# A hybrid GLA and pooling block on one core: column tiles 4 and 5 of r as a second Strassen unit, the feature sums begun earlier

## The chip, the core and the metric

The kernel runs on one core of a Trainium2 chip. The core has a matrix engine (TensorE; PE in the profile, its weight loads PEld), a vector engine (VectorE; DVE), a scalar engine (ScalarE; ACT), GpSimd (POOL) and a sync engine (SyncE; SP) that here issues the DMA transfers. The engines run beside each other and wait for one another at semaphores. SBUF is the on-chip memory with 128 partitions; PSUM is the accumulator memory of TensorE, used here as eight banks of 128 x 512 floats.

The metric is the device time of one execution in microseconds (us), as the median of several runs. The kernel before takes 1376.15 us (three runs: 1376.15, 1376.6 and 1376.02).

## The reference

One transformer-like block on a sequence of 1024 tokens with 1024 channels, in float32:

```python
h = rmsnorm(x, norm_mix)
q, k, v, r, lr_f, lr_b, u, g_a, g_b = split(h @ w_in)        # r: 1024 columns, u: 512, gates: 1024 each
o = gla_forward(q, k, v, decay(lr_f)) + gla_backward(q, k, v, decay(lr_b))   # 4 heads
o = per_head_rmsnorm(o) * gla_norm
o = o * silu(r)
y_a = o @ w_branch_gla
y_b = grouped_linear(multiscale_pool(u)) * pool_scale
merged = sigmoid(g_a) * y_a + sigmoid(g_b) * y_b
x = x + merged @ w_out
gate, up = split(rmsnorm(x, norm_ffn) @ w_ffn_in)
x = x + (silu(gate) * up) @ w_ffn_out
return rmsnorm(x, norm_final)
```

The change lies in the projection h @ w_in, in how the columns of r are computed, and in the preparation of h for it.

## The kernel before

**Numbers as pairs.** Every float32 operand of a matmul is held as two parts, hi (the value cast to the matmul's format) and lo (the rest). A product of two operands is three matmuls, hi x hi, hi x lo and lo x hi (`products`, `mm3`, line 273 does all of them). ScalarE makes hi by a cast (L200) and VectorE or GpSimd makes lo by a subtraction (L201). `hT` is h transposed, features on partitions: for four pairs of k-tiles and two token halves a slot of hi and a slot of lo (`hh`, `hl` in the profile).

**Straight tiles.** `feature_major` computes one column tile of 128 columns for one half of the tokens (512): 8 k-tiles x 3 matmuls, so 48 for both halves. `order` lists the weight tiles that are used this way: q and k of each head, then column tiles 0 to 5 of r. `fetch`, `prepare` and `take` load them, split them and hand them out.

**Strassen units.** Other columns of w_in are computed in units of two column tiles (`Unit`, L1069), as a 2 x 2 block product by Strassen's method in Winograd's form: seven products of 4 k-tiles x 3 matmuls instead of eight. The weights of a unit are two loads of 512 KB (`fraw`), their four combined sums are made on VectorE (`fs`, L1089), and `step(p)` splits the operand of product p. On the other side stand blocks of hT (products 1, 2, 3) and four sums of blocks (products 4 to 7). Products 1, 6, 7, 4 accumulate in one bank, 5 and 3 in another, 2 in a third; after products 1, 6 and 5 ScalarE copies a bank out (`ga`, L1467), and the results of 2, 3, 7, 4 come from VectorE additions to these copies. Before, `gate_units` has 11 units: one of r (column tiles 6 and 7), two of u, four of each gate. `Ahead` prepares the weight operands in the order of use; `R_RUN` is the order of products of the unit of r, 1, 2, 6, 5, 3, 7 and 4, of which 4 is done during the next unit.

**The feature sums.** The four sums of blocks of hT are made early and parked in DRAM. `feature_sums(c)` (L643) restores h from hi + lo on VectorE, takes differences, and stores them to `f_out`; `feature_parts` (L665) loads each back (`hs`), ScalarE casts it (`trh`, L707) and VectorE takes the rest (`trl`, L698). Both run as jobs of `prepare_beside`, which starts one step each `every` units of `mm3` work (one unit is one `mm3` of 512 columns), and only while no weight split is pending. Stores of sums go out three steps after they were made (`PUT`).

**What sets the order.** Each engine executes in the order in which the program issues. The schedule is written out by hand: `pump`, called after every `mm3`, advances first steps put off (`soon`), then weight splits, then `aside` (the jobs beside), then `side` (generators: normalization, transposing features, attention). `finish_side` and `finish_beside` drain these queues. In `first_qk` (L1035) the second half of the tokens is still being transposed in `side` while the first half of q and k is computed; then `low_rank(1)` is run and the feature sums are begun.

**Gated output.** `gated(j, half, src)` (L1178) takes a column tile of r: silu on ScalarE (`sr`), four transposes of the attention output into a bank (`tp`, L1184), and one VectorE instruction that multiplies them into `oT`. After four such calls on a pair of column tiles the two slots of oT are stored. The attention output of heads 0 to 2 was stored to DRAM and is loaded back by `load_o(h)` (`ol`, L1033, two slots of 512 KB); head 3's is still in SBUF. r tiles 0 to 2 are copied out (`whole_r`) and gated later by `put_by`, one half at a time, since the attention of head 3 is then not done.

**Slots.** All large tiles (hT, sums, `fraw`, `ol`, `oT`, `ga`, `trh`, `trl`) come from one pool of 39 slots of 128 x 1024 floats, handed out in turn. An instruction that writes a new tile waits until every user of the slot's former tile is done. SP issues its DMAs in program order, so a load that waits for a slot holds back those behind it.

In the stage of the change the kernel runs: the last attention steps beside r tiles 0 to 3, r tiles 3 to 5 with `put_by` and `gated`, then the loop over `gate_runs` (L1515). The functions and loops named here follow.

Of the kernel before, what the change touches and what calls it, by code (L numbers as in the profile page):

```python
# [53 lines left out]
def kernel(  # L54
# [42 lines left out]
    def slot(dtype=F32, shape=(2, HALF), s="slot"):  # L97
        return slots.tile([P, *shape], dtype, tag="slot", name=name(s))
# [136 lines left out]
            return tuple(t[:, k % self.per, :] for t in self.parts[k // self.per])  # L235


    order = []
    for h in range(HEADS):
        order += [(w_in, KT, c + h * DK, DK) for c in (Q0, K0)]  # L240
    order += [(w_in, KT, R0 + j * P, P) for j in range(KT - 2)]
    order = iter(order)
    loaded, ready = [], []

# [398 lines left out]
    def feature_sums(c):  # L643
# [18 lines left out]
        yield job  # L662
        yield diff(b21, b21, b22, 4)

    def feature_parts():  # L665
        todo = [(p, c) for p in (6, 5, 7, 4) for c in range(2)]
        wholes = []

        def load_sum():
            if len(wholes) < len(todo):  # L670
                p, c = todo[len(wholes)]
                wholes.append(slot(s="hs"))
                nc.sync.dma_start(wholes[-1][:, :, :], f_out[p][:, c])

        yield load_sum, None, None
        for n, (p, c) in enumerate(todo):
            yield load_sum, wholes[n][:, :, :], p

    def parts_for(src):
# [350 lines left out]
    def load_o(h):  # L1030
        o_heads[h] = [slot(shape=(4, DV), s="ol") for _ in range(2)]
        for half in range(2):
            nc.sync.dma_start(o_heads[h][half][:, :, :], o_out[h][:, 4 * half : 4 * half + 4, :])  # L1033

    def first_qk():  # L1035
        q, k = slot(s="q"), slot(s="k")
        low_rank(0)
        weights = [take()]
        for half in range(2):
            if half:  # L1040
                finish_side()
                low_rank(1)
                prepare_beside([feature_sums(0)], 2)
                prepare_beside([feature_sums(1)], 4)
                prepare()
            for n, (dst, scale) in enumerate(((q, DK**-0.5), (k, 1.0))):
                if n == len(weights):
                    weights.append(take(ahead=False))
                ps = feature_major(weights[n], hT, half)
                nc.scalar.activation(dst[:, half, :], ps[:, :], AF.Copy, scale=scale)  # L1050
        qk_heads[0] = q, k
# [104 lines left out]
    def product(unit, p, ps, right):  # L1156
# [6 lines left out]


    ob_out = {(i, half): dram.tile([P, 4, HALF], F32, name=f"ob_out{i}{half}") for i in range(2) for half in range(2)}
    gate_units = [(R0 + 6 * P, R0 + 7 * P)] + [(U0 + 2 * i * P, U0 + (2 * i + 1) * P) for i in range(2)]
    gate_units += [(c0 + 2 * i * P, c0 + (2 * i + 1) * P) for c0 in (GA0, GB0) for i in range(KT // 2)]
    gunits = [Unit(w_in, cols) for cols in gate_units]
    gate_runs = [run_of(n, 0) for n in range(len(gate_units))]
    gate_runs[0] = [(0, p) for p in R_RUN[:-1]]  # L1170
    gate_runs[-1] = last_run(len(gate_units) - 1)
    gates_ahead = Ahead(
        gunits, [(0, p) for p in R_RUN] + list(chain(*(steps_of(n, n == len(gate_units) - 1) for n in range(1, len(gate_units)))))
    )

    raw_r, oT = [], {}
# [27 lines left out]
            gated(*raw_r.pop(0))  # L1204

    BY = 3
    sums_begun = False
    for j in range(KT - 2):
        if 2 <= j <= 4:
            load_o(j - 2)  # L1210
        w = take()
        if j == 4:
            for _ in range(2):
                gunits[0].load()
        if j == 5:
            gates_ahead.step()
        if j < BY:
            whole_r = slot(s="r")
        for half in range(2):
            if j >= BY and not sums_begun and (j > BY or not side):  # L1220
                finish_side()
                finish_beside()
                prepare_beside([feature_parts()], 5)
                sums_begun = True
            ps = feature_major(w, hT, half)
            if half == 0:
                flush()
            if j < BY:
                nc.scalar.copy(whole_r[:, half, :], ps[:, :])
                raw_r.append((j, half, whole_r[:, half, :]))  # L1230
            else:
                put_by()
                gated(j, half, ps[:, :])
            if j == KT - 3 and half == 0:
                gates_ahead.step()
    for p, i, half in ((1, 0, 0), (2, 1, 0), (3, 1, 1)):
        right[p] = [hT.pair(2 * i + c, half) for c in range(2)]

# [206 lines left out]
    class Gates:  # L1445


        def __init__(self, n):
            self.unit = gunits[n]
            self.kind, self.at = next((kind, n - at) for kind, at in (("b", 7), ("a", 3), ("u", 1), ("r", 0)) if n >= at)  # L1450
            self.rows, self.done = [], []

        def row(self, i):
# [4 lines left out]
        def run(self, p):  # L1458
            while len(right.get(p, ())) < 2:
                next(aside[0][0])  # L1460
            ps = bank_of(self, p)
            product(self.unit, p, ps, right)
            ps = ps[:, :]
            finish_late()
            part = {1: (0, 0), 6: (0, 1), 5: (1, 1)}.get(p)
            if part:
                nc.scalar.copy(self.row(part[0])[:, part[1], :], ps)  # L1467
                return
            i, half = {2: (0, 0), 3: (0, 1), 4: (1, 0), 7: (1, 1)}[p]
            done = self.row(i)[:, half, :]  # L1470
            if p != 4:
                add(done, ps, done)
                ps = done
            if self.kind == "r":
                if p == 4:
                    nc.scalar.copy(done, ps)
                late.append(partial(gated, KT - 2 + i, half, done))
                return
            if self.kind != "u":
                nc.scalar.activation(done, ps, AF.Sigmoid)  # L1480
            elif p == 4:
                nc.scalar.copy(done, ps)
            self.done.append((i, half))
            if self.kind == "b" and p in (7, 4):
                for at in self.done:
                    self.pooling(*at)
                self.done = []
# [27 lines left out]
    for n, run in enumerate(gate_runs):  # L1515
        zs[n] = Gates(n)
        last = n == len(gate_units) - 1
        if n == 1:
            prepare_beside(map(output_jobs, range(4)), 2.8)
        if n == 8:  # L1520
            finish_side()
            finish_beside()
            prepare_beside(map(unit_jobs, range(READY)), 2.8, 0, 2)
        for at, (of, p) in enumerate(run):
            if not gates_ahead.step() and at in (5, 7):
                line_make()
            zs[of].run(p)
            for _ in range(2 * (at == 0 and not last)):
                gunits[n + 1].load()
            if p in (7, 4):  # L1530
                zs[of].store(int(p == 4))
            if at == 4:
                flush()
                if n == 3:
                    begin(pooling(), 4)
            if 6 <= n < 10 and at == 5:
                load_pool_weights(n - 6)
            elif n >= 7 and at == 2:
                split_pool_weights(n - 7)
            if n >= 7 and at == (0 if last else 2):  # L1540
                load_pooled(n - 7)
            if last and at == 1:
                finish_beside()
                load_block(0, 0)
# [581 lines left out]
```

## Time and profile before

| | |
|---|---|
| median of three runs | 1376.15 us (1376.02 to 1376.6) |
| profiled execution | 1376.22 us |
| its span in the trace | 1374.5 us |
| TensorE busy in the span | 1363.3 us (99%), 6310 matmuls and transposes |
| VectorE | 832.4 us (61%) |
| ScalarE | 646.6 us (47%) |
| GpSimd | 756.4 us (55%) |
| stretch 0 to 60 us, TensorE busy | 57.75 us |
| stretch 60 to 320 us | 258.79 of 260 us |
| stretch 320 to 356 us (straight tiles of r) | 36.00 of 36 us |
| stretch 356 to 370 us (unit of r) | 13.23 of 14 us |
| stretch 370 to 1374 us | 997.49 of 1004 us |

The span is the time between the first and the last recorded instruction; the execution's time has 1.7 us more around it. In the profile's rows, L and a number is a line of the kernel; `out<-in` are tile names; a timeline row has the start and the duration in us, and in brackets the idle time before the instruction with the engine and tile that ended it. A group row has the count, busy us, mean ns of one, and the idle time before them.

### The profile page before, as it was taken

What the parts mean: (1) busy time and instruction counts of PE and PEld (TensorE: products, weight loads), DVE (VectorE), ACT (ScalarE), POOL (GpSimd) and SP (SyncE); (2) the same over time, 40 slices, a digit from 0 to 9 for tenths busy, and PEclk for the clock granted to TensorE, in tenths of its full rate; (3) what the DMA queues carried; (4) which work ended last, traced back from release to release, by engine and by line L of the source; (5) the groups of instructions that cost most, each with busy time, mean ns of one, the idle gap of its engine ahead of it and who ended that gap; (6) DMA issues with size and microseconds to landing.
All of it is one profiled execution on the core that took longest, in us unless ns stands there. A gap on an engine that the chain in (4) does not pass through costs nothing. (4 is left out here: it accounts for less than half of the span.)

```text
span 1374.5 us, 17888 instructions
## 1 busy us (share of the span) xinstructions
PE 1363.3 (99%) x6310; PEld 1133.5 (82%) x6310; DVE 832.4 (61%) x1034; ACT 646.6 (47%) x1177; POOL 756.4 (55%) x557
## 2 busy tenths in 40 slices
PE   9999999999999999999999999999999999999998
PEld 7878888888888888888888888888888888888886
DVE  6684656554625777678883955655566556343375
ACT  7355766755434445554346533333333334444253
POOL 3231825222597547668764376666676667455454
PEclk9999999999999999999999999999999999999999
DMA  7132414323778569996416355555544447985561
GB/s 227 54 100 77 145 68 147 112 66 123 241 238 275 183 206 304 373 383 216 154 66 242 114 176 176 176 176 176 174 144 137 146 136 251 384 321 184 169 215 77
DMA packets 167834, 251.97 MB, mean 183 GB/s; under 512 B 11160, under 2 KB 94144, under 8 KB 167744
## 3 DMA queue, kind: packets, MB, share of 16 engines
q1 hardware_dynamic: 167600, 250.57, 54.1%
q8 instruction: 49, 0.80, 0.2%
q14 instruction: 41, 0.34, 0.1%
q10 hardware_dynamic: 144, 0.26, 0.1%
HBM read 168.74 MB, written 82.05 MB: 182 GB/s over the span
## 5 line engine op out<-in xcount | busy, mean ns | idle before, releaser
L201 POOL TENSOR_TENSOR wl<-fs,wh 128x512 fp32r<-128x512 f32 x124 | 173.0, 1400 | 162.4 <-ACT wh L200 106.2
L273 PE MATMUL ps<-gh,wh 128*128 128x512 f32 x616 | 240.5, 390 | 0.0
L273 PE MATMUL ps<-gl,wh 128*128 128x512 f32 x616 | 239.8, 389 | 0.3 <-DVE gl L1684 0.3
L273 PE MATMUL ps<-gh,wl 128*128 128x512 f32 x616 | 239.7, 389 | 0.0
L201 POOL TENSOR_TENSOR wl<-fraw,wh 128x512 fp32r<-128x512 f32 x93 | 134.1, 1442 | 75.9 <-ACT wh L200 70.2
L201 POOL TENSOR_TENSOR ol<-gor,oh 128x1024 fp32r<-128x1024 f32 (+1 forms) x42 | 101.3, 2416 | 86.1 <-ACT oh L200 60.0
L273 PE MATMUL ps<-hh,wh 128*128 128x512 f32 x356 | 145.3, 408 | 0.8 <-ACT ga L1467 0.8
L273 PE MATMUL ps<-hh,wl 128*128 128x512 f32 x356 | 139.0, 391 | 0.0
L273 PE MATMUL ps<-hl,wh 128*128 128x512 f32 x356 | 138.8, 390 | 0.0
L273 PEld LDWEIGHTS ps<-gh,wh 128*128 128x128 f32 x616 | 115.7, 188 | 24.3 <-ACT hb L1703 0.3
L273 PEld LDWEIGHTS ps<-gl,wh 128*128 128x128 f32 x616 | 115.7, 188 | 24.2 <-DVE gl L1684 0.7
L273 PEld LDWEIGHTS ps<-gh,wl 128*128 128x128 f32 x616 | 115.7, 188 | 23.9
L273 PE MATMUL ps<-oh,ol 128*128 128x512 f32 x308 | 119.9, 389 | 0.0
L273 PE MATMUL ps<-ol,oh 128*128 128x512 f32 x308 | 119.8, 389 | 0.0
L273 PE MATMUL ps<-oh,oh 128*128 128x512 f32 x308 | 119.8, 389 | 0.0
L201 POOL TENSOR_TENSOR wl<-wraw,wh 128x512 fp32r<-128x512 f32 x56 | 93.3, 1696 | 43.7 <-ACT wh L200 43.6
L201 DVE TENSOR_TENSOR ol<-wor,oh 128x1024 fp32r<-128x1024 f32 (+1 forms) x42 | 62.4, 1497 | 69.5 <-ACT oh L200 57.0
L201 POOL TENSOR_TENSOR wl<-raw,wh 128x512 fp32r<-128x512 f32 x34 | 47.5, 1410 | 100.4 <-ACT wh L200 93.0
L200 ACT CAST wh<-fs 128x512 fp32r<-128x512 f32 x124 | 76.1, 615 | 29.8 <-DVE fs L1089 28.8
L273 PEld LDWEIGHTS ps<-hh,wl 128*128 128x128 f32 x356 | 66.8, 188 | 14.5
L273 PEld LDWEIGHTS ps<-hh,wh 128*128 128x128 f32 x356 | 67.0, 188 | 13.2 <-ACT ga L1467 1.2
L273 PEld LDWEIGHTS ps<-hl,wh 128*128 128x128 f32 x356 | 67.0, 188 | 12.1
(281 smaller groups left out, 3074.1 us busy)
## 6 DMA issues: line engine op xcount, KB each, us to landing
fraw<-in_w_ffn_in_dram SPq DMA_DIRECT2D x44, 512.0 KB, 6.7
gor<-g_out SPq DMA_DIRECT2D x35, 512.0 KB, 5.5
fraw<-in_w_in_dram SPq DMA_DIRECT2D x22, 512.0 KB, 6.4
g_out<-s SPq DMA_DIRECT2D x44, 256.0 KB, 2.3
wor<-t_out SPq DMA_DIRECT2D x20, 512.0 KB, 3.9
raw<-in_w_in_dram SPq DMA_DIRECT2D x36, 256.0 KB, 4.0
g_out<-g SPq DMA_DIRECT2D x33, 256.0 KB, 2.6
x<-in_x_dram SPq DMA_DIRECT2D x16, 512.0 KB, 5.3
```

The costliest lines, as they stand in the source:

```text
L200: nc.scalar.copy(hi, src)
L201: eng.tensor_tensor(lo, src, as_f32(hi), op=ALU.subtract)
L273: nc.tensor.matmul(ps, a[i], b[j], start=first and n == 0, stop=last and n == 2, skip_group_check=onto)
```

## The change

Column tiles 4 and 5 of r leave `order` and become a second unit (`R_UNITS = 2`), so that there are 12 units; the indices of the later units' extra work move up by one. The straight tiles are 0 to 3. The second unit's products run as 1, 2, then product 4 of the first, then 6, 5, 3, 7, and its own 4 in the first unit of u. Because tile 3 is the last straight one, only two of the six put-off halves of r are gated beside it; the other four are gated after the first four products of the first unit. `load_o(0)` and `load_o(1)` stay before tiles 2 and 3, and `load_o(2)` comes after product 2. The units' weights are loaded before tile 2 and after tile 3.

The feature sums are begun by a generator placed in `side` behind the last features, during the first half of q and k, both at a pace of 2 steps; they were begun after `low_rank(1)`, at 2 and 4. The sums' return (`feature_parts`) begins in the second half of tile 3 or earlier, at a pace of 2.8 instead of 5, and its first loads are issued in a group of three after the first half of tile 3 instead of by a job of its own.

```diff
--- before.py
+++ after.py
@@ -235,10 +235,11 @@
             return tuple(t[:, k % self.per, :] for t in self.parts[k // self.per])
 
 
+    R_UNITS = 2
     order = []
     for h in range(HEADS):
         order += [(w_in, KT, c + h * DK, DK) for c in (Q0, K0)]
-    order += [(w_in, KT, R0 + j * P, P) for j in range(KT - 2)]
+    order += [(w_in, KT, R0 + j * P, P) for j in range(KT - 2 * R_UNITS)]
     order = iter(order)
     loaded, ready = [], []
 
@@ -662,18 +663,17 @@
         yield job
         yield diff(b21, b21, b22, 4)
 
+    part_order = [(p, c) for p in (6, 5, 7, 4) for c in range(2)]
+    wholes = []
+
+    def load_sum():
+        if len(wholes) < len(part_order):
+            p, c = part_order[len(wholes)]
+            wholes.append(slot(s="hs"))
+            nc.sync.dma_start(wholes[-1][:, :, :], f_out[p][:, c])
+
     def feature_parts():
-        todo = [(p, c) for p in (6, 5, 7, 4) for c in range(2)]
-        wholes = []
-
-        def load_sum():
-            if len(wholes) < len(todo):
-                p, c = todo[len(wholes)]
-                wholes.append(slot(s="hs"))
-                nc.sync.dma_start(wholes[-1][:, :, :], f_out[p][:, c])
-
-        yield load_sum, None, None
-        for n, (p, c) in enumerate(todo):
+        for n, (p, c) in enumerate(part_order):
             yield load_sum, wholes[n][:, :, :], p
 
     def parts_for(src):
@@ -1032,6 +1032,10 @@
         for half in range(2):
             nc.sync.dma_start(o_heads[h][half][:, :, :], o_out[h][:, 4 * half : 4 * half + 4, :])
 
+    def sums_behind():
+        prepare_beside(map(feature_sums, range(2)), 2)
+        yield 0
+
     def first_qk():
         q, k = slot(s="q"), slot(s="k")
         low_rank(0)
@@ -1040,9 +1044,9 @@
             if half:
                 finish_side()
                 low_rank(1)
-                prepare_beside([feature_sums(0)], 2)
-                prepare_beside([feature_sums(1)], 4)
                 prepare()
+            else:
+                begin(sums_behind())
             for n, (dst, scale) in enumerate(((q, DK**-0.5), (k, 1.0))):
                 if n == len(weights):
                     weights.append(take(ahead=False))
@@ -1163,14 +1167,17 @@
 
 
     ob_out = {(i, half): dram.tile([P, 4, HALF], F32, name=f"ob_out{i}{half}") for i in range(2) for half in range(2)}
-    gate_units = [(R0 + 6 * P, R0 + 7 * P)] + [(U0 + 2 * i * P, U0 + (2 * i + 1) * P) for i in range(2)]
+    gate_units = [(R0 + j * P, R0 + (j + 1) * P) for j in range(KT - 2 * R_UNITS, KT, 2)]
+    gate_units += [(U0 + 2 * i * P, U0 + (2 * i + 1) * P) for i in range(2)]
     gate_units += [(c0 + 2 * i * P, c0 + (2 * i + 1) * P) for c0 in (GA0, GB0) for i in range(KT // 2)]
     gunits = [Unit(w_in, cols) for cols in gate_units]
     gate_runs = [run_of(n, 0) for n in range(len(gate_units))]
     gate_runs[0] = [(0, p) for p in R_RUN[:-1]]
+    gate_runs[1] = [(1, 1), (1, 2), (0, 4)] + [(1, p) for p in R_RUN[2:-1]]
     gate_runs[-1] = last_run(len(gate_units) - 1)
     gates_ahead = Ahead(
-        gunits, [(0, p) for p in R_RUN] + list(chain(*(steps_of(n, n == len(gate_units) - 1) for n in range(1, len(gate_units)))))
+        gunits, [(n, p) for n in range(R_UNITS) for p in R_RUN]
+        + list(chain(*(steps_of(n, n == len(gate_units) - 1) for n in range(R_UNITS, len(gate_units)))))
     )
 
     raw_r, oT = [], {}
@@ -1204,35 +1211,41 @@
             gated(*raw_r.pop(0))
 
     BY = 3
+    LAST = KT - 2 * R_UNITS - 1
     sums_begun = False
-    for j in range(KT - 2):
-        if 2 <= j <= 4:
+    for j in range(LAST + 1):
+        if j >= 2:
             load_o(j - 2)
         w = take()
-        if j == 4:
+        if j == LAST - 1:
             for _ in range(2):
                 gunits[0].load()
-        if j == 5:
+        if j == LAST:
             gates_ahead.step()
         if j < BY:
             whole_r = slot(s="r")
         for half in range(2):
-            if j >= BY and not sums_begun and (j > BY or not side):
+            if j >= BY and not sums_begun and (half or not side):
                 finish_side()
                 finish_beside()
-                prepare_beside([feature_parts()], 5)
+                prepare_beside([feature_parts()], 2.8)
                 sums_begun = True
             ps = feature_major(w, hT, half)
             if half == 0:
                 flush()
+            elif j == LAST:
+                for _ in range(2):
+                    gunits[1].load()
             if j < BY:
                 nc.scalar.copy(whole_r[:, half, :], ps[:, :])
                 raw_r.append((j, half, whole_r[:, half, :]))
             else:
                 put_by()
                 gated(j, half, ps[:, :])
-            if j == KT - 3 and half == 0:
+            if j == LAST and half == 0:
                 gates_ahead.step()
+                for _ in range(3):
+                    load_sum()
     for p, i, half in ((1, 0, 0), (2, 1, 0), (3, 1, 1)):
         right[p] = [hT.pair(2 * i + c, half) for c in range(2)]
 
@@ -1447,7 +1460,7 @@
 
         def __init__(self, n):
             self.unit = gunits[n]
-            self.kind, self.at = next((kind, n - at) for kind, at in (("b", 7), ("a", 3), ("u", 1), ("r", 0)) if n >= at)
+            self.kind, self.at = next((kind, n - at) for kind, at in (("b", 8), ("a", 4), ("u", 2), ("r", 0)) if n >= at)
             self.rows, self.done = [], []
 
         def row(self, i):
@@ -1474,7 +1487,7 @@
             if self.kind == "r":
                 if p == 4:
                     nc.scalar.copy(done, ps)
-                late.append(partial(gated, KT - 2 + i, half, done))
+                late.append(partial(gated, LAST + 1 + 2 * self.at + i, half, done))
                 return
             if self.kind != "u":
                 nc.scalar.activation(done, ps, AF.Sigmoid)
@@ -1515,9 +1528,9 @@
     for n, run in enumerate(gate_runs):
         zs[n] = Gates(n)
         last = n == len(gate_units) - 1
-        if n == 1:
+        if n == 2:
             prepare_beside(map(output_jobs, range(4)), 2.8)
-        if n == 8:
+        if n == 9:
             finish_side()
             finish_beside()
             prepare_beside(map(unit_jobs, range(READY)), 2.8, 0, 2)
@@ -1525,20 +1538,24 @@
             if not gates_ahead.step() and at in (5, 7):
                 line_make()
             zs[of].run(p)
-            for _ in range(2 * (at == 0 and not last)):
+            if n == 0:
+                put_by()
+                if at == 1:
+                    load_o(2)
+            for _ in range(2 * (at == 0 < n and not last)):
                 gunits[n + 1].load()
             if p in (7, 4):
                 zs[of].store(int(p == 4))
             if at == 4:
                 flush()
-                if n == 3:
+                if n == 4:
                     begin(pooling(), 4)
-            if 6 <= n < 10 and at == 5:
-                load_pool_weights(n - 6)
-            elif n >= 7 and at == 2:
-                split_pool_weights(n - 7)
-            if n >= 7 and at == (0 if last else 2):
-                load_pooled(n - 7)
+            if 7 <= n < 11 and at == 5:
+                load_pool_weights(n - 7)
+            elif n >= 8 and at == 2:
+                split_pool_weights(n - 8)
+            if n >= 8 and at == (0 if last else 2):
+                load_pooled(n - 8)
             if last and at == 1:
                 finish_beside()
                 load_block(0, 0)
```

## The prediction

> **What bounds the kernel now.** I read the page first: busy shares, granted clock, chain of waits.
>
> ```profile
> span 1374.5 us, 17888 instructions
> ...
> PE 1363.3 (99%) x6310; PEld 1133.5 (82%) x6310; DVE 832.4 (61%) x1034; ACT 646.6 (47%) x1177; POOL 756.4 (55%) x557
> ...
> PEclk9999999999999999999999999999999999999999
> ...
> PE 44%; DVE 1%; ACT 1%; issue 0%; POOLq 0%; POOL 0%; DVEq 0%; ACTq 0%
> ```
>
> TensorE is busy 99% of the span at full clock; no other engine passes 61%. So time is the number of matmuls times their pitch, plus the few places where TensorE waits. The pitch is not the mean of the groups. I took it from busy time by stretches (length; then busy us and instructions of PE, PEld, DVE, ACT, POOL; clock; DMA share; GB/s), and beside it one group by line with shapes kept apart:
>
> ```profile
> 356.00:370.00 14.00, 13.23 (x60) 10.59 (x59) 11.66 (x11) 6.88 (x11) 11.31 (x7) 1.00 0.89 290
> 800.00:900.00 100.00, 100.00 (x443) 82.84 (x442) 54.69 (x56) 34.37 (x63) 69.85 (x52) 1.00 0.48 155
> ...
> L273 PE MATMUL ps<-hh,wl 128*128 128x512 f32 x356 | 139.0, 391 | 0.0
> ```
>
> 443 matmuls in 100 us are 0.2257 us each, while one lasts 391 ns: they overlap, and a removed matmul is worth 0.226 us and not 0.39. The first row is the stretch of the present Strassen unit of r, where TensorE is idle for 14.00 - 13.23 = 0.77 us. Its timeline there:
>
> ```profile
> 364.67 0.39 PE L273 MATMUL ps<-trh,wl 128*128 128x512 f32 x1
> ...
> 365.20 0.58 ACT L1467 COPY ga<-ps 128x512 f32<-128x512 f32 x1
> ...
> 365.83 0.50 PE L273 MATMUL ps<-hh,wh 128*128 128x512 f32 x1 [0.77 <-ACT ga L1467]
> ```
>
> Product 5 starts its last matmul at 364.67, ScalarE copies its bank out from 365.20 to 365.78, and product 3, which accumulates in the same bank, starts at 365.83. Of 1.16 us between the starts, 0.93 are lost (1.16 - 0.23). That is the price of "5 then 3" in R_RUN.
>
> The early waits come from VectorE, in the timelines of both engines:
>
> ```profile
> 57.10 0.69 DVE L553 TENSOR_TENSOR lrT<-ps,lrT 32x512 fp32r<-32x512 f32 x1 [11.32 <-ACT lrT L552]
> ...
> 97.20 1.41 DVE L492 TENSOR_TENSOR vl<-ps,vh 128x256 fp32r<-128x256 f32 x4
> ...
> 99.12 1.21 DVE L713 TENSOR_TENSOR hs<-hh,hl 128x1024 f32<-128x1024 f32 x1
> ...
> 97.03 0.28 PE L273 MATMUL kv<-vh,kt 128*128 128x256 f32 x1
> ...
> 97.67 0.39 PE L273 MATMUL kv<-vl,kt 128*128 128x256 f32 x1 [0.35 <-DVE vl L492]
> ...
> 98.58 0.40 PE L273 MATMUL ps<-hh,wl 128*128 128x512 f32 x1
> ...
> 99.26 0.39 PE L273 MATMUL kv<-vh,kt 128*128 128x256 f32 x1 [0.28 <-DVE kt L201]
> ...
> 99.48 0.28 PE L273 MATMUL kv<-vl,kt 128*128 128x256 f32 x1
> 99.60 0.28 PE L273 MATMUL kv<-vh,kt 128*128 128x256 f32 x1
> ...
> 100.19 0.39 PE L273 MATMUL ps<-hh,wl 128*128 128x512 f32 x1
> ...
> 100.88 0.36 PE L273 MATMUL kv<-vh,kt 128*128 128x256 f32 x1 [0.30 <-DVE st L911]
> ...
> 112.61 0.28 PE L273 MATMUL op<-vl,p 128*128 128x256 f32 x1
> ...
> 113.11 0.38 PE L273 MATMUL op<-vh,p 128*128 128x256 f32 x1 [0.23 <-DVE p L201]
> ```
>
> VectorE stands idle for 11.32 us before 57.10 and is late for TensorE at 97 to 113 while it still makes feature sums (99.12). Against a pitch of 0.12 after a 256-column matmul (99.48 to 99.60) and 0.23 after one of 512, the four gaps lose 0.64 - 0.12, 0.68 - 0.23, 0.69 - 0.23 and 0.50 - 0.12: 1.81 us.
>
> **Part 1, matmuls.** A straight column tile is 8 k-tiles x 3 products x 2 halves = 48 matmuls, two are 96. A Strassen unit is 7 products x 4 k-tiles x 3 = 84. So 12 go: 12 x 0.2257 = 2.71 us, all on the engine that sets the end. The transposes of gated() stay 64. The unit adds to ScalarE three weight casts and four copies out of PSUM, to GpSimd three weight differences, to VectorE four weight sums and three additions; the products cover that work as long as these engines have room: in the present unit's 14.00 us VectorE is busy 11.66, GpSimd 11.31 and ScalarE 6.88 (the row above), so VectorE comes closest to the bound, which part 5 prices. The weights' bytes stay the same: four loads of 256 KB become two of 512 KB.
>
> **Part 2, feature sums begun earlier.** They now follow the last features into the side queue, so VectorE's idle 11.32 us take them. They are eight restorations and eight differences, of which these rows give the price:
>
> ```profile
> L713 DVE TENSOR_TENSOR hs<-hh,hl x8: 1212/1218/2304, 57.8 to 99.1; 128x1024 f32<-128x1024 f32 x8
> L713 DVE TENSOR_TENSOR hs<-hs,hs x8: 1212/1224/1637, 62.3 to 102.2; 128x1024 f32<-128x1024 f32 x8
> ```
>
> 16 x 1.22 = 19.5 us of VectorE: about nine fit ahead of 57.1, the others into 57.8 to 69, where the first eight ran before. Those that ran between 76 and 102 are then gone from the place where VectorE is late. Their stores move up on SP's queue with them; nothing on it is due before the next head's weights. Bounds: 0 (the attention chain is late for another reason) to -1.81. I take -1.8, because the row that delays 100.88 stands directly behind a feature sum.
>
> **Part 3, "5 then 3" twice.** Two units with R_RUN's order pay it twice. In the first, a put-off column's four transposes now stand between the products and fill about 0.4 us (four transposes are half of this row); in the second nothing does.
>
> ```profile
> 333.52 1.04 PE L1184 MATMUL tp<-ident,ol 128*128 128x128 f32 x8
> ```
>
> That is 0.53 + 0.93 against 0.93 before: +0.5. Bounds 0 to +0.9.
>
> **Part 4, slots.** The pool has 39. SP's timeline and waits, then who waited in ScalarE's, show that it is full in this stage already:
>
> ```profile
> 318.02 26.02 SPq L673 DMA_DIRECT2D hs<-f_out  x4
> SPq L673 <- PE tp L1184: 14.0, 1, 14.0
> SPq L673 <- DVE trl L698: 9.1, 1, 9.1
> 347.33 1.05 ACT L707 CAST trh<-hs 128x1024 fp32r<-128x1024 f32 x1 [5.18 <-PE tp L1184]
> L1033 SPq DMA_DIRECT2D ol<-o_out x6: 339/384/814, 267.3 to 311.9; - x6
> DMA to landing us min/median/max: 4.2/4.2/4.2
> ```
>
> Feature loads waited 14.0 us for a transpose to free a slot and 9.1 for a split. It cost TensorE nothing, since straight tiles followed. Now count what is held after product 2 of the first unit in the changed order: 12 of hT; 2 of head 3's o; 2 of r; 3 of heads 0 and 1's o; 4 of oT; 1 and 2 of the units' raw weights; 1 of ga; 5 of hs; 7 of trh and trl: 39. So load_o(2), which stands there, gets its two slots only from the put-off column just gated. TensorE's order from there is: transposes, product 6 (12 x 0.2257 = 2.71), then the transposes of column 4, which read the first of these loads. The load lands 4.2 us after its issue. With the slot freed by the transposes themselves, TensorE loses 4.2 - 2.7 = 1.5 us. If the slot is r's, its silu waits on ScalarE behind a feature cast (1.05, above) and the casts and copies of the unit; if the last hs load stands ahead of load_o(2) on SP, it waits for a trl on VectorE. Each adds 1 to 2.5, and a 512 KB load in front adds transfer time: up to 6 in all. Queued behind the waiting transposes are products 5, 3 and 7, and so everything. I take 3.0, one ScalarE delay above the lower bound. Bounds +1.5 to +6, and 0 if the count is wrong (a rival).
>
> **Part 5, feature splits at a pace of 2.8 and not 5.** The first must be there 4 to 5 mm3 steps (0.68 us each) after its difference is issued, where it had some 20 steps before. The work itself:
>
> ```profile
> L707 ACT CAST trh<-hs x8: 1040/1052/1058, 328.9 to 360.9; 128x1024 fp32r<-128x1024 f32 x8
> L698 DVE TENSOR_TENSOR trl<-hs,trh x8: 1211/1222/2317, 335.6 to 367.1; 128x1024 fp32r<-128x1024 f32 x8
> 358.77 2.32 DVE L698 TENSOR_TENSOR trl<-hs,trh 128x1024 fp32r<-128x1024 f32 x1
> 355.30 6.94 POOL L201 TENSOR_TENSOR wl<-fs,wh 128x512 fp32r<-128x512 f32 x4 [4.04 <-ACT wh L200]
> ```
>
> Between product 1 and product 6 there are 5.4 us of matmuls; VectorE owes two weight sums, two gatings and two trl: some 7 us with those it is behind by, less what may lie before. At 1.22 a trl it is in time; at 2.32, as beside GpSimd, the second is late by some tenths. I take +0.2, bounds 0 to +1.5. The Trainium skill ("SBUF — State Buffer", section Who interferes with whom) says that a VectorE instruction with two SBUF inputs and a GpSimd one that reads SBUF exclude each other for a whole instruction. The 2.32 beside the GpSimd row agrees; if every trl and weight sum paid that, this term would be its bound, +1.5, and the sum 1376.7.
>
> **Sum.** The profiled execution took 1376.22 (span 1374.5, 1.7 around it), 0.07 from the median 1376.15 of three runs. 1376.22 - 2.71 - 1.8 + 0.5 + 3.0 + 0.2 = 1375.4.
>
> **Rivals.**
> 1. *Nothing is late.* The slots suffice or load_o(2) is early enough: parts 4 and 5 are 0, part 3 is +0.5. 1376.22 - 2.71 - 1.8 + 0.5 = 1372.2. For it: TensorE hardly waits anywhere in this stage before, and SP ran some 20 us ahead of it. Against: the 39, and the 14.0 us wait.
> 2. *Slower: ScalarE stands in the queue for a slot.* Casts trh of the later sums take slots that only the store of oT frees. Before, a cast stood 5.18 us, harmless among straight tiles. Behind it now lie the copies of products 1, 6 and 5 out of PSUM, for which products 6, 7 and 3 wait. On top of part 4 another 5.2: 1375.4 + 5.2 = 1380.6. It decides from the point where a cast waits longer than one product, 2.7 us. For it: the pool is full to the last slot after product 2, and ScalarE takes one of the 39 for every cast. Against: the freed four slots of hT, and part 4's stall gives the store time to land.
> 3. *The early move does nothing.* Part 2 is 0: 1377.2. For it: VectorE is nearly full from 57 to 97. Against: 11.32 us of idle time.
> 4. *A matmul is worth its 0.39.* Then 12 save 4.7 and the forecast would be 1373.4; the 443 in 100 us speak against it.
>
> **Numbers.** Chances: forecast 0.46 (part 4 between 1.5 and 6, time 1374 to 1378.5), rival 1 0.30, rival 2 0.14, rival 3 0.07, rival 4 0.03. A measurement of this kernel tells about 0.2% (2.75 us) from no change. Rivals 1 and 4 and a little of the forecast's lower edge lie below 1373.4: faster 0.36. Rival 2 and the forecast's upper edge lie above 1378.9: slower 0.19. The rest, 0.45, is the same. The range goes from just under rival 1, 1371.6, to 1379.0, past the upper bound of part 4; the forecast's own is 1374 to 1378.5.
>
> **What would show it.** Part 1: 12 matmuls fewer. Part 2: no feature sum after 75 us, and no wait of TensorE on VectorE between 95 and 115. Part 3: two gaps of about a microsecond ahead of product 3. Part 4: a gap of 1.5 to 6 us ahead of a transpose of tp in the first unit, ended by the load of ol; SP's issue of it after the transposes of the column before. Part 5: trl named as releaser of a product 6. The prediction is wrong if load_o(2) lands before product 6 ends, or if VectorE is late at 97 as before.

## The result and the profile after

The changed kernel takes 1387.46 us (median of six runs, 1387.26 to 1387.55) against 1376.09 us of the kernel before in the same session: 11.4 us slower, ratio 1.0082 with a 95% interval from 1.0071 to 1.0092. The profiled execution has a span of 1385.7 us. The forecast was 1375.4 and its range ended at 1379.0.

The first page and the table by stretches of the changed kernel (length; then busy us and instructions of PE, PEld, DVE, ACT, POOL; granted clock; DMA share; GB/s) show the place of the loss:

```profile
span 1385.7 us, 17876 instructions
...
PE 1364.2 (98%) x6298; PEld 1133.8 (82%) x6298; DVE 847.7 (61%) x1041; ACT 651.3 (47%) x1184; POOL 758.0 (55%) x560
...
320.00:345.00 25.00, 17.76 (x89) 14.35 (x87) 18.35 (x24) 13.65 (x21) 11.27 (x7) 0.93 0.55 174
345.00:356.00 11.00, 7.67 (x29) 6.18 (x29) 6.70 (x6) 6.61 (x10) 2.54 (x2) 0.81 0.24 99
356.00:372.00 16.00, 16.00 (x72) 13.10 (x71) 10.33 (x12) 6.39 (x11) 6.18 (x6) 0.92 0.31 92
```

Twelve matmuls are gone (6310 to 6298), as said. But in the stage of the two units TensorE stands idle for 10.6 us (7.24 to 345 us, 3.33 to 356), and the granted clock is below 1, where the kernel before has 1.00 throughout. The loss lies in this stage alone: matched matmul by matmul, the changed kernel is 0.9 us ahead of the kernel before at 327 us, 11.4 us behind it at 400 us, and still 11.4 at 1300 us. The timeline of the two units (start, duration, in brackets the idle time before and what ended it), TensorE first, then the other engines in the first unit:

```profile
333.06 0.60 PE L1191 MATMUL tp<-ident,ol 128*128 128x128 f32 x4
334.33 0.50 PE L274 MATMUL ps<-trh,wh 128*128 128x512 f32 x1 [0.67 <-ACT ga L1480]
...
344.12 1.94 PE L1191 MATMUL tp<-ident,ol 128*128 128x128 f32 x8 [6.57 <-DMA ol<-o_out]
345.71 0.78 PE L274 MATMUL ps<-trh,wh 128*128 128x512 f32 x1
346.29 0.63 PE L274 MATMUL ps<-trl,wh 128*128 128x512 f32 x1
...
348.36 0.40 PE L274 MATMUL ps<-trh,wh 128*128 128x512 f32 x1
...
353.66 0.50 PE L274 MATMUL ps<-hh,wh 128*128 128x512 f32 x1 [3.33 <-ACT ga L1480]
...
355.18 0.63 PE L274 MATMUL ps<-hh,wh 128*128 128x512 f32 x1
...
358.56 0.39 PE L274 MATMUL ps<-trh,wl 128*128 128x512 f32 x1
...
377.27 0.50 PE L274 MATMUL ps<-hh,wh 128*128 128x512 f32 x1 [0.73 <-ACT ga L1480]
```

```profile
333.69 0.59 ACT L1480 COPY ga<-ps 128x512 f32<-128x512 f32 x1 [0.27 <-PE tp L1191]
...
336.46 1.66 DVE L698 TENSOR_TENSOR trl<-hs,trh 128x1024 fp32r<-128x1024 f32 x1
...
338.18 0.80 SPq L1033 DMA_DIRECT2D ol<-o_out  x2
...
346.16 1.22 DVE L698 TENSOR_TENSOR trl<-hs,trh 128x1024 fp32r<-128x1024 f32 x1 [5.65 <-PE tp L1191]
...
347.42 1.04 ACT L707 CAST trh<-hs 128x1024 fp32r<-128x1024 f32 x1 [5.83 <-DVE trl L698]
...
350.70 2.23 DVE L698 TENSOR_TENSOR trl<-hs,trh 128x1024 fp32r<-128x1024 f32 x1
...
353.02 0.59 ACT L1480 COPY ga<-ps 128x512 f32<-128x512 f32 x1 [1.57 <-DVE trl L698]
```

Read them as one chain. SP can issue the load of head 2's output only at 338.18, when VectorE has finished the difference that began at 336.46 (338.12), because that difference frees its slot. The transposes of column tile 4 wait 6.57 us for it. Meanwhile VectorE and ScalarE stand too: VectorE's next difference needs a slot that these queued transposes free (5.65 us), and ScalarE's next cast a slot that this difference frees (5.83 us). They are 6 us behind when TensorE goes on, and the copy of product 5's bank, which also needs a new slot, waits for the difference of 350.70 to end at 352.93; product 3 waits 3.33 us for the copy. The copy of product 1's bank had stood behind two casts on ScalarE and then waited 0.27 us for a transpose to free its slot (0.67 us for TensorE). The second unit has only the wait before its product 3 that the kernel before has too (0.73).

After each of the two long waits the matmuls last 0.63 us instead of 0.39. From 345.71 to 348.36 are six matmul starts and from 355.18 to 358.56 eight: 2.65 and 3.38 us where 0.227 each would be 1.36 and 1.82.

### The profile page after: what moved, and what is told of

Its sections match the earlier page's. It is cut to its first block, busy times and chain, and to the rows that moved or that the text cites. A ratio compares the mean times of both kernels' runs of the same rounds, so it can differ in the third digit from the quotient of the medians.

```text
span 1385.7 us, 17876 instructions
## 1 busy us (share of the span) xinstructions
PE 1364.2 (98%) x6298; PEld 1133.8 (82%) x6298; DVE 847.7 (61%) x1041; ACT 651.3 (47%) x1184; POOL 758.0 (55%) x560
## 5 line engine op out<-in xcount | busy, mean ns | idle before, releaser
L201 POOL TENSOR_TENSOR wl<-fs,wh 128x512 fp32r<-128x512 f32 x128 | 178.0, 1396 | 172.4 <-ACT wh L200 116.1
L201 POOL TENSOR_TENSOR wl<-fraw,wh 128x512 fp32r<-128x512 f32 x96 | 138.7, 1444 | 90.2 <-ACT wh L200 87.6
L274 PE MATMUL ps<-hh,wh 128*128 128x512 f32 x336 | 137.8, 410 | 4.1 <-ACT ga L1480 4.1
L274 PE MATMUL ps<-hh,wl 128*128 128x512 f32 x336 | 131.7, 392 | 0.0
L274 PE MATMUL ps<-hl,wh 128*128 128x512 f32 x336 | 131.5, 392 | 0.0
L201 POOL TENSOR_TENSOR wl<-raw,wh 128x512 fp32r<-128x512 f32 x30 | 41.6, 1398 | 80.8 <-ACT wh L200 63.1
L274 PE MATMUL ps<-trh,wh 128*128 128x512 f32 x192 | 76.0, 396 | 0.7 <-ACT ga L1480 0.7
L274 PEld LDWEIGHTS ps<-hh,wh 128*128 128x128 f32 x336 | 63.4, 189 | 16.0 <-ACT ga L1480 4.7
L274 PE MATMUL ps<-trl,wh 128*128 128x512 f32 x192 | 75.5, 393 | 0.0
```

The costliest lines, as they stand in the source:

```text
L201: eng.tensor_tensor(lo, src, as_f32(hi), op=ALU.subtract)
L274: nc.tensor.matmul(ps, a[i], b[j], start=first and n == 0, stop=last and n == 2, skip_group_check=onto)
```

## The experiments

**The early sums alone.** The kernel before with this edit:

```diff
-                prepare_beside([feature_sums(0)], 2)
-                prepare_beside([feature_sums(1)], 4)
                 prepare()
+            else:
+                begin(sums_behind())
```

> The kernel before with the early feature sums alone. Theory 'given back': the trace of the changed kernel has no wait of TensorE between 95 and 115 us, 2.0 us less than before, but four new ones of 0.4 us each at 166.7, 173.6, 174.3 and 237.6 us, 1.6 us in all; if these come with the earlier sums, they are here too and the time is 1375.7 (-0.4). Rival 'they belong to the second unit': then this kernel has none of them and the time is 1374.3 (-1.8), the term of the prediction.

Measured: 1375.51 us against 1376.09 (ratio 0.9994, 95% interval 0.9985 to 1.0002; brackets below hold the same). The list of what TensorE waited for between 90 and 250 us (total, times, longest), first in the kernel before, then here:

```profile
PE kv L273 <- DVE vl L492: 0.4, 1, 0.4
PE kv L273 <- DVE st L911: 0.3, 1, 0.3
PE kv L273 <- DVE kt L201: 0.3, 1, 0.3
PE op L273 <- DVE p L201: 0.2, 1, 0.2
```

```profile
PE ps L273 <- POOL wl L201: 0.6, 1, 0.6
PE op L273 <- DVE p L201: 0.4, 2, 0.2
PE op L273 <- ACT p L200: 0.3, 1, 0.3
```

The waits that the prediction priced are gone, and others have come. The gain is 0.6 us, and its interval reaches no gain at all. Matched matmul by matmul, the two traces show the giving back itself: this kernel is 3.0 us ahead from 118 to 165 us, 1.2 at 183 us and 0.7 from 240 us on. The theory "given back" holds.

**The second unit alone.** The changed kernel with the sums begun where they were (the edit above undone).

> The changed kernel with the feature sums begun where they were before. Theory: the whole loss lies in the stage of the two units, so the stall ahead of the transposes of column tile 4 is there with 6.7 us and the one ahead of product 3 with some 3.6, and the time is that of the changed kernel plus what the early sums are worth, 1387.9 (+0.4). Rival 'earlier sums fill the queues': if their earlier stores and VectorE's work shifted the later stage, the stalls shrink here by more than 1 us and the time is under 1386.

Measured: 1389.33 us (1387.3 to 1390.12). TensorE waits 6.4 us for the load and up to 2.8 us for ScalarE's copies in the same places, so the loss lies in the units, and the rival is out. That it is 1.9 us slower than the changed kernel and not 0.4 was not expected. From 355 to 360 us, behind the second wait, the granted clock is 0.50 here (13 matmuls) and 0.66 in the changed kernel (17), so the slow stretch lasted longer. Matched matmul by matmul, this profiled run (1390.12 us) is behind that of the changed kernel (1387.43) by 1.1 us before the stage, by another 1.1 at this slow stretch, and by 0.5 after it.

**Gating sooner.** The changed kernel with

```diff
             else:
                 put_by()
+                put_by()
                 gated(j, half, ps[:, :])
```

> The changed kernel with two put-off halves gated after each half of tile 3 instead of one, so that two slots of r and two of the attention output come free before the first unit instead of in it. Theory 'slots': the load of head 2's output gets a free slot without waiting for VectorE or ScalarE and lands before product 6 ends; the stall of 6.7 us is under 1, with it the slow matmuls behind it (2.7 us in both places) go at least in the first place, and the time is 1376 to 1380. Rival 'SP's queue': the load is late because it stands behind the loads of the feature sums in SP's order; these go on waiting for VectorE's differences, and the stall stays above 4 us and the time above 1384.

Measured: 1379.32 us (1377.27 to 1380.0), 8.1 us less. TensorE's waits in the stage, and SP's timeline:

```profile
PE tp L1191 <- DMA ol<-o_out: 2.7, 1, 2.7
PE ps L274 <- ACT ga L1481: 1.4, 2, 0.7
PE ps L274 <- DVE trl L698: 0.4, 1, 0.4
```

```profile
330.71 4.28 SPq L673 DMA_DIRECT2D hs<-f_out  x3
335.10 0.85 SPq L1033 DMA_DIRECT2D ol<-o_out  x2
```

Four slots freed earlier take away most of the wait for ScalarE (3.33 to 0.7) and most of the wait for the load. Of the 2.7 us that stay SP's order has about 2: the last load of a feature sum still waits 2.1 us for a transpose to free its slot, and head 2's load stands behind it; once issued, that load takes 6.0 us until the transposes start, where the prediction had 4.2. So both theories have a part, the slots the larger one. The edit also moves two gatings' work on ScalarE and VectorE out of the first unit, but these engines were not short of time there: in the changed kernel they stand idle for 5.83 and 5.65 us, for slots. The trace is that of an execution of 1377.27 us with a mean granted clock of 0.999; the runs near the median have 0.997 to 0.998. That points to slow matmuls behind the wait in them too, but no trace shows it.

**TensorE kept busy through the wait.** The changed kernel with, in `gated`,

```diff
         tp = bank(ps_g, "tp")
+        if (j, half) == (4, 0):
+            for i in range(56):
+                nc.tensor.transpose(tp[:, i % 4 * P : (i % 4 + 1) * P], ident[:, :], ident[:, :])
```

> The changed kernel with 56 more transposes of the unit matrix, into the bank that the real ones overwrite, ahead of the transposes of column tile 4, first half. They fill the wait of 6.6 us (56 x 0.11 = 6.2 us) and do nothing else. Theory 'clock': the matmuls after the wait lasted 0.63 us instead of 0.39 because TensorE's clock fell during it; with TensorE busy the stretch 345 to 348 us runs at 0.39, its loss of 1.2 us and that of its transposes, 0.9, go, and the second slow stretch, after the idle of 3.3 us, stays: 1385.4 to 1386.5. Rival 'contention': the matmuls were slow for a port or a transfer at that time; they stay at 0.63 and the time at 1387.5.

Measured: 1390.22 us (1389.55 to 1391.12), 2.8 us slower, where both theories had it no slower. By stretches, first the changed kernel, then this one; and this one's timeline:

```profile
345.00:350.00 5.00, 5.00 (x20) 4.19 (x20) 1.97 (x2) 2.58 (x5) 0.00 (x0) 0.67 0.23 93
```

```profile
345.00:350.00 5.00, 3.56 (x20) 2.77 (x18) 1.23 (x1) 0.94 (x1) 0.00 (x0) 1.00 0.32 128
```

```profile
344.27 1.09 PE L1194 MATMUL tp<-ident,ol 128*128 128x128 f32 x8 [0.37 <-DMA ol<-o_out]
345.12 0.48 PE L274 MATMUL ps<-trh,wh 128*128 128x512 f32 x1
345.44 0.39 PE L274 MATMUL ps<-trl,wh 128*128 128x512 f32 x1
...
347.80 1.23 DVE L698 TENSOR_TENSOR trl<-hs,trh 128x1024 fp32r<-128x1024 f32 x1 [7.11 <-DMA ob_out<-o]
...
356.22 0.79 PE L274 MATMUL ps<-hh,wh 128*128 128x512 f32 x1 [7.66 <-ACT ga L1483]
```

On the clock the run is clear: with TensorE busy the stretch behind the wait runs at 1.00 and 0.39 us a matmul, and the same eight transposes take 0.85 us to the next start (344.27 to 345.12) instead of 1.59. The rival "contention" is out, since the DMAs moved more in that stretch (128 GB/s against 93). The time can't tell what the clock alone costs, because another wait changed with the edit: VectorE's difference now waited for a slot that the store of oT freed (7.11 us), and the wait before product 3 grew from 3.33 to 7.66 us.

**Head 2's load sooner.** The changed kernel with

```diff
-                if at == 1:
-                    load_o(2)
...
+    load_o(2)
     for p, i, half in ((1, 0, 0), (2, 1, 0), (3, 1, 1)):
```

> The changed kernel with one edit: the load of head 2's attention output is issued at the end of tile 3, ahead of the first unit, instead of after its second product. Theory 'place': there it stands ahead of the loads that wait on SP, takes slots that hT's tiles left, and lands before the transposes; the stall of 6.7 us and the slow matmuls behind it go (1.2 us, and 0.9 in the transposes), but the pool stays as full, so that ScalarE's copies and casts still wait for slots of feature sums and a stall of 2 to 4 us stays before product 3: 1378 to 1381. Rival 'the pool alone decides': whatever is placed first, some other tile is late by the same; a stall of 5 us or more comes up at another place of the first unit and the time stays above 1384.

Measured: 1386.0 us (1385.09 to 1386.36), only 1.5 less. TensorE's waits:

```profile
PE ps L274 <- ACT ga L1481: 7.5, 3, 5.0
PE ps L274 <- DVE trl L698: 2.7, 1, 2.7
```

SP's issue of the load:

```profile
322.02 0.81 SPq L1033 DMA_DIRECT2D ol<-o_out  x2
```

The load is no longer waited for, and nearly the same time is lost elsewhere: 5.0 us before product 3, 2.7 us for a difference and 1.8 us for the copy of product 1's bank. The rival "the pool alone decides" holds. Placing one tile first makes the next ones late.

**Both.** Gating sooner and the load sooner together.

> The changed kernel with both: two put-off halves gated after each half of tile 3, and head 2's load issued at the end of tile 3. In the run with the earlier gating alone the load's slots were free, and it stood behind a feature sum's load that waited for a transpose; 2.9 us were left. Theory 'slots, then SP's order': now neither waits; no gap over 1.2 us in the first unit, the 2.9 us go and the time is 1375 to 1376.5. Rival 'VectorE': its differences at a pace of 2.8 are then the next bound, with a stall over 1.5 us ahead of a product of the feature sums, and the time stays at 1377 to 1379.

Measured: 1375.23 us (0.9991, 0.9982 to 1.0). What is left of TensorE's waits is 1.4 us for the copies ahead of the two products 3 and 1.1 us for VectorE's differences, none over 0.73. The theory "slots, then SP's order" holds: with the slots free the load's place counts. The kernel is now level with the kernel before (0.9 us less by the medians, with an interval that reaches 1.0).

**Product 7 ahead of product 3**, on top of both, and alone in the kernel before:

```diff
-    R_RUN = 1, 2, 6, 5, 3, 7, 4
+    R_RUN = 1, 2, 6, 5, 7, 3, 4
```

> The same with product 7 ahead of product 3 in the order of the two units of r, so that ScalarE copies product 5's bank while product 7 runs. Theory: the gaps ahead of product 3 (0.84 and 0.89 us in the run with the earlier gating) go and nothing else changes: 1.7 us less than without, 1373.5 to 1375. Rival: the sums for product 7 are needed 2.7 us sooner and VectorE is late with them; a gap ahead of product 7 takes the place of the one ahead of 3 and the time is that of the run without this edit.

> The kernel before with product 7 ahead of product 3 in its one unit of r, to measure the disputed term by itself. By the trace of before the copy of product 5's bank costs 0.93 us: 1375.2. Rival: the wait is hidden by or moves to a later one: 1376.1.

Measured: 1374.06 us (0.9985, 0.9976 to 0.9994) and 1375.04 us (0.9992, 0.9984 to 1.0001). The wait before product 3 is gone in both. Alone it is worth 1.1 us, where the trace had 0.93; the interval just reaches no gain, but matched matmul by matmul the whole 1.1 us appears at this place. In the two units it brings 1.2 us where 1.7 was expected, and VectorE takes a part back: its difference is 0.36 us late for product 7.

**The jobs behind the sums held back.** After the line that queues the sums of w_branch:

```diff
             prepare_beside(map(branch_jobs, range(4)), 4.2)
+            aside[-1][1] += 32
```

> The kernel before with the early feature sums, and the jobs that come behind them in the same queue (the sums of w_branch, on GpSimd) held back by 32 steps of mm3. With the early sums alone these jobs began with their first load at 84.6 us instead of 106.5, GpSimd ran one of them at 162.97 us ahead of a weight split that TensorE waited for at 166.95 us, and the early gain was given back there. Theory 'the jobs behind moved up': held back to where they were (22 us are 32 steps of 0.68), the waits at 167 to 238 us are gone and the gain of 1.8 us stands: 1374.3. Rival 'the attention chain itself': the waits belong to the earlier attention steps and stay: 1375.5, as with the early sums alone.

> The kernel with both moves and product 7 ahead of 3, with the same jobs held back by 32 steps. Theory 'the jobs behind moved up': its four waits between 166 and 238 us, 1.6 us, go and the time is 1372.5. Rival: they stay, or others take their place: 1374.1.

Measured: 1373.67 us (0.9982, 0.9973 to 0.9991) and 1372.26 us (0.9972, 0.9961 to 0.9982). The loads of these jobs by tile in the kernel before, with the early sums alone, and held back:

```profile
L597 SPq DMA_DIRECT2D wsum<-in_w_branch_gla_dram x8: 368/405/652, 106.5 to 209.1; - x8
```

```profile
L597 SPq DMA_DIRECT2D wsum<-in_w_branch_gla_dram x8: 367/405/559, 84.6 to 185.2; - x8
```

```profile
L597 SPq DMA_DIRECT2D wsum<-in_w_branch_gla_dram x8: 384/423/503, 147.3 to 207.2; - x8
```

The 32 steps held them longer than meant, to 147 us and not 106, so this is not the old place but a third one. Still the waits for GpSimd's split and ScalarE's cast are gone, of the list above only VectorE's `p` stays (0.4 us in two), and the early sums are worth 2.4 us instead of 0.6. The same matmul in the three traces, by its start in us, shows where:

| kernel before | early sums alone | held back |
|---|---|---|
| 95.30 | 95.26 | 95.28 |
| 120.01 | 116.98 | 117.01 |
| 160.56 | 157.52 | 157.54 |
| 181.86 | 180.68 | 179.58 |
| 249.92 | 249.23 | 247.91 |

Up to 160 us both have gained the same 3.0 us. Then the early sums alone give back 2.3 of them and the kernel with the jobs held back 1.0. So the jobs that moved up had taken more than half of what was given back; why 1.0 us still goes was not tested. The second of these two kernels is the fastest of all, 3.9 us under the kernel before.

**One slot less**, in the changed kernel and in the kernel before (`SLOTS = 38`).

> The changed kernel with a pool of 38 slots instead of 39. Theory 'the pool is full': every tile of the first unit takes a slot that comes free one allocation later, and the gaps of the first unit, 6.7, 3.6 and 0.9 us, grow in sum by 1 us or more: 1388.5 to 1395. Rival 'order on SP and pace on VectorE': one slot changes nothing there and the time stays within 0.5 us of 1387.5.

> The kernel before with 38 slots, the other half of the comparison. Both theories: straight tiles follow in that stage and cover a late load, so TensorE has no new gap over 1 us between 320 and 372 us; the later stages may cost up to 1 us: 1376 to 1377.

Measured, one run each: 1399.8 and 1382.99 us. TensorE's longest waits in the stage, of the changed kernel with 38 slots, then of the kernel before with 38:

```profile
PE ps L274 <- ACT ga L1480: 8.3, 3, 7.3
PE tp L1191 <- DMA ol<-o_out: 6.8, 1, 6.8
```

```profile
363.42 0.50 PE L273 MATMUL ps<-trh,wh 128*128 128x512 f32 x1 [2.26 <-ACT ga L1467]
```

A slot is worth 12.3 us to the changed kernel, more than the 1388.5 to 1395 us expected, and of that some 4 lie in this stage (its waits were 6.6 and 4.7 us with 39); the rest lies outside it. The expectation for the kernel before was wrong: it too gets a wait of 2.26 us here, and others outside, 6.9 us in all. It stood at the edge of its pool already; the change stepped over it.

## Why the prediction was wrong

| term | forecast, us | measured, us |
|---|---|---|
| 12 matmuls | -2.71 | -2.71 (12 fewer; the price is not measured here, see below) |
| early sums | -1.8 | -0.6 (the run alone; in the changed kernel's own trace 0.9 ahead at 327 us) |
| idle time in the units: slots, "5 then 3", VectorE's pace | +0.5 + 3.0 + 0.2 | 6.57 + 3.33 + 0.67 + 0.73 - 0.77 = +10.5 |
| clock after the waits | not in the sum | 1.29 + 0.74 + 1.56 = +3.6 |
| sum | -0.8 | +10.8, against +11.4 |

The idle times leave out a little at each wait: the prediction's 0.77 us of idle time was 0.93 from start to start. Some 0.16 us at each of four waits is an estimate of the 0.6 us that are missing.

**Slots, the step that failed.** The place was right, and the count of 39 is borne out: the load of head 2 waits for a slot, and the transposes of column 4 for the load, for 6.57 us where 1.5 to 6 had been given and 3.0 taken. What failed is "I take 3.0, one ScalarE delay above the lower bound". The lower bound had the load issued when the transposes of the column before end, at 333.66. SP issued it at 338.18, 4.5 us later: 2.6 us because the last load of a feature sum stood ahead of it, and 1.9 us for VectorE's difference. The prediction had named the first and priced it at 1 to 2.5; in place of the second it had a delay on ScalarE, and it counted one of the two. And the load took 5.9 us until the transposes started, not 4.2. Behind this step stands the idea that a full pool makes one tile late. Every tile written after that point takes a slot that has only just come free, on whichever engine writes it: the copies out of PSUM, the casts and the differences. While TensorE stood at the load, VectorE and ScalarE stood behind TensorE, and the second wait, 3.33 us before product 3, followed. That the pool is the cause is shown by three runs: four slots freed sooner take 8.1 us away, moving the load alone only 1.5, and one slot less adds 12.3, some 4 of them in this stage.

**The clock** was left out. Two waits of 6.57 and 3.33 us were each followed by a stretch at a lower clock: 1.29 us in the first's matmuls, 1.59 - 0.85 = 0.74 in its transposes and 3.38 - 1.82 = 1.56 in the second. The run that kept TensorE busy shows the cause for the first. These are parts of TensorE's time and not what a full clock would have given back: the chain from the transposes to the copy of product 5's bank (346.16 to 353.02 in the rows above) runs through VectorE and ScalarE, so without the 1.29 us in product 5 the wait before product 3 would have been longer by as much. A stall of the size that the prediction allowed, up to 6 us, should have been given a price for the clock as well.

**Early sums.** They fit into VectorE's idle time and the waits of 97 to 113 us went. That was worth 3.0 us by 118 us, more than the 1.81 of the four gaps that the prediction counted. The step that failed is "nothing on it is due before the next head's weights": SP's queue was looked at, but not the queue of jobs beside, where the sums of w_branch stand behind the feature sums and moved up by 22 us into GpSimd's weight splits. Held back they leave 2.4 us.

**"5 then 3" twice.** In the second unit 0.73 us of idle time, as before. In the first it can't be told from the slot wait, which is ended by the same copy. The kernel before with the other order has the size, 1.1 us alone.

**A matmul's worth.** The fastest kernel bears on it. Without the units, the early sums held back (1373.67) and the other order (-1.1) would give 1372.6 if their gains add. With them it is 1372.26, and TensorE waits 1.4 us for VectorE's differences in the first unit. Taken from start to start, against the usual pitch, these gaps and one of 0.32 behind the first transposes lose 2.3 us (0.63, 0.90 and 0.48 for the three). 2.7 saved less 2.3 is 0.4, where 0.3 is seen. A price of 0.39 per matmul (4.7 us) would leave 2.4 and does not fit. The profiled runs, matched matmul by matmul, show even less: the stage is 0.95 us shorter with the units and the other order, and 1.1 with the order alone.

**VectorE's pace** of 2.8 is no cause in the changed kernel, but it is what is late next: the three waits of the fastest kernel in this stage are all for `trl`:

```profile
334.53 0.50 PE L274 MATMUL ps<-trl,wh 128*128 128x512 f32 x1 [0.35 <-DVE trl L698]
...
340.30 0.50 PE L274 MATMUL ps<-trl,wh 128*128 128x512 f32 x1 [0.74 <-DVE trl L698]
...
343.67 0.50 PE L274 MATMUL ps<-trl,wh 128*128 128x512 f32 x1 [0.32 <-DVE trl L698]
```

**The rivals.** "Nothing late" came near only when the gating and the load were both moved. The slower rival had the right kind of cause, ScalarE standing in the queue for a slot, and one of its three places, the wait of product 3. Wrong were the size (5.2 us) and what frees the slot, the store of oT: in the changed kernel the slots came from VectorE's differences, and the store of oT decided only in the run with TensorE kept busy.

## What to carry to other kernels

When a pool of buffers is full at one point of the program, count not the one load that comes late there but every tile that is allocated until the pool has slack again, on each engine that writes one; the cure is to release earlier, and moving a single load forward mostly passes the wait on. A job that is moved up in a queue moves up everything behind it, so price what follows at its new place too. And a stall of some microseconds on TensorE can cost more than its length: behind the 3.33 us here went another 1.56.

## What was unexpected of the hardware

TensorE's granted clock fell after idle times of 6.57 and 3.33 us in the changed kernel, of 2.79 us with the second unit alone and of 2.75 us with head 2's load sooner. After 2.73 us in the profiled run with sooner gating and 2.26 us in the kernel before with 38 slots it stayed at 1.00. The run with the second unit alone has the fall at its fullest, 0.50 (timeline, then the stretch):

```profile
354.69 0.79 PE L274 MATMUL ps<-hh,wh 128*128 128x512 f32 x1 [2.79 <-ACT ga L1480]
355.28 0.63 PE L274 MATMUL ps<-hl,wh 128*128 128x512 f32 x1
```

```profile
355.00:360.00 5.00, 5.00 (x13) 3.84 (x13) 4.68 (x5) 2.23 (x4) 2.20 (x2) 0.50 0.26 107
```

The traces' record of the granted clock puts order into this. It is either 1.00 or 0.50, and in each trace the instants at which it changes lie whole multiples of 3.41 us apart. It is 0.50 from 341.44 to 348.27 and from 355.10 to 358.51 us in the changed kernel, from 353.86 to 360.68 around the end of the 2.79 us, and from 344.61 to 354.85 with head 2's load sooner. What decides, as far as these traces show, is how much of a wait falls into one such stretch of 3.41 us. In the stretch ahead of these four falls TensorE was idle for 3.41, 1.98, 1.96 and 2.48 us. The 2.73 us that brought no fall were split, 1.20 us in one stretch and 1.53 in the next, and no stretch with 1.85 us or less brought one in any trace here. So a wait of the same length can be followed by slow matmuls or not, by its place.

The Trainium skill ("TensorE: Matmul & The Clock Gate", Part 1: The HAM clock gate) has the half clock after an idle window of about 3.4 us, the windows running on by themselves. The half clock and the regular stretches agree; the idle time that brought it here was shorter, 1.96 us within a stretch.
